# A gated feed-forward layer by seven products: gate/up parts named one product ahead, and nine block pairs instead of ten

## The chip, the cores and the metric

The kernel runs on one core of a Trainium2 chip. The metric is device time in microseconds for one execution of the whole program, a two-layer decoder trunk. Below, PE is the matrix engine, DVE the vector engine, ACT the scalar engine, POOL the general one (its queue also issues transfers), and SP the queue that issues most transfers.

## What is computed

Two layers, each a token mixer followed by a dense gated feed-forward (FFN); pre-normalisation before each, plain residual adds, one final normalisation. The prompt has 1024 tokens and there are 8 single decode tokens, so every matrix product runs over 1032 columns. All is float32. The part that the change touches, cut to what matters:

```python
D_MODEL = 1024
D_FF = -(-8 * D_MODEL // (3 * 256)) * 256          # 2816 = 22 blocks of 128

def swiglu(x, w_gate_up, w_down):
    g, u = jnp.split(x @ w_gate_up, 2, axis=-1)
    return (jax.nn.silu(g) * u) @ w_down

for layer in range(DEPTH):                         # layer 0: mLSTM mixer, layer 1: latent attention
    ...                                            # mixer, residual add
    hp = hp + swiglu(rmsnorm(hp, norm_ffn[layer]), ffn_w_gate_up[layer], ffn_w_down[layer])
    hs = hs + swiglu(rmsnorm(hs, norm_ffn[layer]), ffn_w_gate_up[layer], ffn_w_down[layer])
y_prompt = rmsnorm(hp, norm_final)
```

## The kernel before

**Precision.** A float32 operand is split into a rounded high half and the rest (`split`: ACT writes the high half, DVE subtracts for the low half), and each product is three matmuls: high x high, high x low, low x high (`mm3`, lines 134 to 136). So every weight and every activation passes through ACT and DVE before PE can use it.

**Tiling.** The 1032 columns are two parts, i = 0 with 2 x 256 columns and i = 1 with 2 x 260. The hidden dimension is 22 blocks f of 128. `gate_up(wg, f, parts)` makes one block of gated activations `u[f, i]`, as a 2 x 2 block product in seven instead of eight products (`PRODUCTS`). Per product and part it issues 4 x 3 = 12 matmuls into a bank tagged `sc`. The weights' operands of the seven products come from the generator `operands`: two loads of 512 KB (tag `wr`, two buffers, one for gate and one for up), four sums and differences on POOL (tag `S`), and seven splits (`put`). The split parts go to three slots in turn: two of tag `wh` and one of tag `w3`. They are named in the order of the products, each just before the product that uses it, but for one (`s1`) that is named a product early.

**Pairs.** `down` multiplies pairs of blocks (f0, f0 + 1) with the down weights, again by seven products. A pair is four items (two output tiles of 128 each), an item is 14 steps (7 products x 2 parts) of 3 matmuls, in banks `mm` and `ss`. Each item loads its weights (`dr`, 256 KB, on SP), makes sums and differences on DVE (`dS`), splits them (tags `dA` to `dD`), evicts its products into a staging tile, and ends with two accumulating stores into the residual `x_d`, issued by POOL: from the tile `st` (part 1) and from `st0` (part 0), which lies in the two `wl` buffers of the weights' pool. The activations of a pair are combined and split into fourteen tiles `b` by `spread`, at steps listed in `SPREAD`.

**Order.** `ffn` first makes blocks 2, 0 and 1 (0 and 1 for part 0 were made before), then starts the generator `down` and gives it to `gate_up` for blocks 3 to 21: after every second k of a product one step of `down` follows, 28 steps for a block. So from block 3 on, PE alternates six matmuls of gate/up with three of a pair. Ten pairs are done so; the last two blocks, 20 and 21, are kept as split activations `act` and multiplied plainly, with 3 matmuls per block, output tile and column piece, in the tail: `last_products`, called by `to_mla` in layer 0 (three pieces of 344 columns) and by `finish` in layer 1 (384, 384 and 264). The tail loads the down weights of the kept blocks for each of the 8 output tiles (`wr`, 128 KB), splits them, reads the residual back from `x_d`, adds, and goes on to the next layer's operands and squares or to the final normalisation and the output. In layer 1 block 21 is made in two passes, part 0 and part 1, each with its own loads.

The program is traced in this order and placed on the engines' queues by the framework when it is built; each queue then runs in order, with semaphores between engines. A tile's slot in a pool must be read out before its next owner may be written.

**Memory.** Pools are stacks on the left and the right of the on-chip memory. `fp` (left) holds what the pairs need: the `b` tiles, `dr`, `dS`, `dA` to `dD`, `st`, and `w3`. `gu` (right) holds `u`, `gt` and `S`; `fc` (right) the normalised inputs of part 1; `fz` (left) those of part 0.

Of the kernel before, what the change touches and what calls it, by code (L numbers as in the profile page):

```python
# [91 lines left out]
class Kern:  # L92
# [896 lines left out]
    def operands(self, wg, f):  # L989
        nc = self.nc  # L990
        A = []
        for c0 in (f * P, DFF + f * P):
            raw = self.t(self.wp, [P, KT * P], "wr")
            nc.sync.dma_start(raw.rearrange("p (k m) -> p k m", m=P), self.wsrc(wg, 0, KT, c0, P))
            A.append(raw.rearrange("p (k r m) -> p r k m", r=2, m=P))
        (a11, a12), (a21, a22) = ((x[:, 0], x[:, 1]) for x in A)

        def put(x):
            self.no += 1
            pool, tag = (self.wp, "wh") if self.no % 3 else (self.fp, "w3")  # L1000
            w = self.t(pool, [P, KT * P], tag, F32R).rearrange("p (i k m) -> p i k m", i=2, m=P)
            self.split(w[:, 0], w[:, 1], x)
            return w

        G = nc.gpsimd.tensor_tensor
        s, s3 = (self.t(self.gu, [P, 4, P], "S", bufs=2) for i in range(2))
        G(s, a21, a22, op=ALU.add)  # L1007
        G(s3, a11, a21, op=ALU.subtract)
        yield put(a11)
        yield put(a12)  # L1010
        s1 = put(s)
        G(s, s, a11, op=ALU.subtract)  # L1012
        yield put(s)
        yield s1
        G(s, a12, s, op=ALU.subtract)  # L1015
        yield put(s3)
        yield put(a22)
        yield put(s)


    def gate_up(self, wg, f, parts, down=iter(()), skip=0, steps=1):
        nc = self.nc
        V = nc.vector
        gu = self.gu
        banks = {}
        U, X = {}, {}
        for (s, bank, first), w in zip(PRODUCTS, self.operands(wg, f)):
            for i in parts:
                pw = PW[i]
                if (i, bank) not in banks:  # L1030
                    banks[i, bank] = self.mmt("sc")[:, :pw]
                ps = banks[i, bank]
                xh, xl = self.F[i][s]
                for k in range(4):
                    self.mm3(ps, w[:, 0, k], w[:, 1, k], xh[:, k], xl[:, k], bool(first) and k == 0, k == 3, skip_group_check=True)
                    if k % 2:
                        if skip:
                            skip -= 1
                        else:
                            for _ in range(steps):  # L1040
                                next(down, None)
                if s == 0:
                    U[i] = self.rows(f, i)
                    X[i] = self.t(gu, [P, PW[1]], "gt", bufs=2)[:, :pw]
                u, x = U[i], X[i]
                if s == 0:
                    nc.scalar.copy(u[:, 0], ps)
                elif s == 4:
                    V.tensor_tensor(u[:, 0], u[:, 0], ps, op=ALU.add)
                    nc.scalar.activation(u[:, 0], u[:, 0], AF.Silu)  # L1050
                elif s == 3:
                    nc.scalar.copy(x, ps)
                elif s == 2:
                    nc.scalar.copy(u[:, 1], ps)
                    V.tensor_tensor(u[:, 1], u[:, 1], banks[i, 1], op=ALU.add)
                elif s == 5:
                    V.tensor_tensor(u[:, 0], u[:, 0], ps, op=ALU.mult)  # L1057
                elif s == 6:
                    V.tensor_tensor(x, x, ps, op=ALU.add)
                    nc.scalar.activation(x, x, AF.Silu)  # L1060
                    V.tensor_tensor(u[:, 1], u[:, 1], x, op=ALU.mult)
# [42 lines left out]
    def down(self, wd):  # L1104
        nc = self.nc
        V = nc.vector
        todo = [(f0, dp) for f0 in range(0, NF - 2, 2) for dp in range(KT // 2)]
        src = self.down_raw(wd, *todo[0])
        W = {n: self.down_put(src, n) for n in "ABCD"}
        st0 = [self.t(self.wp, [P, KT * P], "wl", F32R).bitcast(F32) for _ in range(2)]  # L1110
        yield
        for n, (f0, dp) in enumerate(todo):
            more = n + 1 < len(todo)
            st, o, banks = [], [], []
            for i in range(2):
                x = st0[dp % 2].rearrange("p (r t) -> p r t", r=2) if i == 0 else self.t(self.fp, [P, 2, 2 * PW[1]], "st", bufs=2)
                st.append(x)
                o.append(x.rearrange("p r (c t) -> p r c t", c=2))
                banks.append([self.mmt(t)[:, :PW[i]] for t in ("mm", "ss")])
            for e in range(14):  # L1120
                s, k, first = PRODUCTS[e // 2]
                i = e % 2
                ps = banks[i][k]
                w, j = PARTS[s]
                w, b = W[w][:, :, j], self.B[s, i]
                self.mm3(ps, w[:, 0], w[:, 1], b[:, 0], b[:, 1], bool(first), True, skip_group_check=True)
                c = o[i]
                if s == 0:
                    nc.scalar.copy(c[:, 0, 0], ps)
                elif s == 4:  # L1130
                    V.tensor_tensor(c[:, 0, 0], c[:, 0, 0], ps, op=ALU.add)
                elif s == 3:
                    nc.scalar.copy(c[:, 0, 1], ps)
                elif s == 2:
                    nc.scalar.copy(c[:, 1, 1], ps)
                    V.tensor_tensor(c[:, 1, 1], c[:, 1, 1], banks[i][1], op=ALU.add)
                elif s == 5:
                    nc.scalar.copy(c[:, 1, 0], ps)
                elif s == 6:
                    V.tensor_tensor(c[:, 0, 1], c[:, 0, 1], ps, op=ALU.add)  # L1140
                    nc.gpsimd.dma_start(self.x_d[:, 2 * dp:2 * dp + 2, 512 * i:512 * i + 2 * PW[i]], st[i], accum_op=ALU.add)  # L1141
                if more and e == 0:
                    src = self.down_raw(wd, *todo[n + 1])
                if more and e in (6, 9, 12, 13):
                    x = {6: "A", 9: "B", 12: "D", 13: "C"}[e]
                    W[x] = self.down_put(src, x)
                for f, z in ((f0, dp * 14 + e + 56), (f0 + 2, dp * 14 + e)):
                    if 0 < f < NF - 2:
                        for when, x, part in SPREAD:
                            if when == z:  # L1150
                                self.spread(f, x, part)
                yield

    def ffn(self, layer):
        wg, wd = self.ffn_w_gate_up[layer], self.ffn_w_down[layer]
        self.fp = self.pool("ffn")
        self.B = {}
        for _, x, i in SPREAD:
            if i == 0:
                self.spread(0, x, i)  # L1160
        self.gate_up(wg, 2, (0, 1))
        self.gate_up(wg, 0, (1,))
        self.gate_up(wg, 1, (1,))
        for _, x, i in SPREAD:
            if i == 1:
                self.spread(0, x, i)
        g = self.down(wd)
        next(g)
        self.gate_up(wg, 3, (0, 1), g, 1, 2)
        for f in range(4, NF - 1):  # L1170
            self.gate_up(wg, f, (0, 1), g)
        fs = range(NF - 2, NF)
        self.act = {}

        def last(pool, tag, i):
            for f in fs:
                if f not in self.act:
                    self.act[f] = [self.t(pool, [P, T], tag(f - NF + 2, x), F32R) for x in range(2)]
                o = lambda x: x[:, 512 * i:512 * i + 2 * PW[i]].rearrange("p (c t) -> p c t", c=2)
                self.split(o(self.act[f][0]), o(self.act[f][1]), self.u[f, i], lo_eng=self.nc.vector)  # L1180

        if layer:
            for i in range(2):
                self.gate_up(wg, NF - 1, (i,), g)
                last(self.fz, lambda j, x: f"f{2 * j + x}l", i)
            self.fc.release()
        else:
            self.gate_up(wg, NF - 1, (0, 1), g)
            self.fc.release()
            self.lt = self.pool("lt", side="right")  # L1190
            for i in range(2):
                last(self.lt, lambda j, x: f"l{j}{x}", i)
        for _ in g:
            pass
        return wd, fs


# [10 lines left out]
    def to_mla(self, wd, fs):  # L1208
# [22 lines left out]
        self.lead = self.ahead(self.load_w(self.wsrc(self.mla_w_in[0], 0, KT, QL, P), KT, P), z, KT, P)  # L1231
        y = self.rms_tok(SS, T)
        tl.release()
        self.lt.release()
        self.gu.release()
        self.fp.release()
        self.rsp = self.pool("rsz")
# [780 lines left out]
```

## Time and profile before

| | us |
|---|---|
| median of 3 runs | 2785.11 (2776.23 to 2789.87) |
| profiled execution | 2787.24 |
| its span, first to last instruction | 2785.5 |
| PE busy in the span | 2579.9 (93%) |
| DVE busy | 1925.7 (69%) |
| ACT busy | 1352.1 (49%) |
| POOL busy | 859.2 (31%) |
| mean granted clock of PE | 0.962 |

The times of the profile are from the start of the span. Layer 0's FFN with its pairs runs from about 564 to 1218 and its tail to about 1263; layer 1's from about 2060 to 2731, and its tail to the end. "Busy" is the union of an engine's instruction times; a busy PE may still run at half its clock, which the granted clock shows (1.00 is full). In a row of waits the first name is the instruction that waited and the second the one that released it; in a row of groups the last number is idle time of that engine just before the group's instructions. Line 118 is the subtraction that makes a low half, line 117 the copy that makes a high half, whoever calls them, so the tile's name tells which it is: `wh`, `w` and `wl` are weights, `b` a pair's activations.

### The profile page before, as it was taken

What the parts mean: (1) busy time and instruction counts of PE and PEld (TensorE: products, weight loads), DVE (VectorE), ACT (ScalarE), POOL (GpSimd) and SP (SyncE); (2) the same over time, 40 slices, a digit from 0 to 9 for tenths busy, and PEclk for the clock granted to TensorE, in tenths of its full rate; (3) what the DMA queues carried; (4) which work ended last, traced back from release to release, by engine and by line L of the source; (5) the groups of instructions that cost most, each with busy time, mean ns of one, the idle gap of its engine ahead of it and who ended that gap; (6) DMA issues with size and microseconds to landing.
All of it is one profiled execution on the core that took longest, in us unless ns stands there. A gap on an engine that the chain in (4) does not pass through costs nothing.

```text
span 2785.5 us, 55009 instructions
## 1 busy us (share of the span) xinstructions
PE 2579.9 (93%) x21199; PEld 2412.7 (87%) x21199; DVE 1925.7 (69%) x4469; ACT 1352.1 (49%) x3403; POOL 859.2 (31%) x778
## 2 busy tenths in 40 slices
PE   8999998889999999989889899888989999999987
PEld 8998977889999999988876767677988999999987
DVE  4345678967777777776558677685777777777776
ACT  4212334445555555553345464555446555555553
POOL 1001002233333333332336454442213333333333
PEclk9999989999999999999989999899999999999998
DMA  5133555327555566663667776555425566555665
GB/s 183 38 76 92 132 142 146 108 62 140 120 116 113 113 120 120 127 173 102 216 220 272 242 257 219 199 202 180 130 75 108 117 121 117 116 113 119 123 129 145
DMA packets 346508, 392.91 MB, mean 141 GB/s; under 512 B 23833, under 2 KB 275102, under 8 KB 337926
## 3 DMA queue, kind: packets, MB, share of 16 engines
q0 software_dynamic: 63872, 191.79, 30.0%
q1 hardware_dynamic: 257974, 181.25, 21.9%
q10 hardware_dynamic: 24400, 16.36, 2.4%
q8 instruction: 166, 2.72, 0.4%
q14 instruction: 96, 0.79, 0.1%
HBM read 255.17 MB, written 134.16 MB: 140 GB/s over the span
## 4 chain that ended last, share of the span: by engine, by line
PE 55%; DVE 24%; DMA 9%; ACT 4%; issue 4%; POOL 3%; SPq 0%; POOLq 0%; DVEq 0%; ACTq 0%
PE sc L136 10%; PE sc L134 10%; PE sc L135 10%; PE mm L134 4%; PE mm L136 4%; PE mm L135 4%; DVE b L118 3%; DVE tt L1796 2%; PE ss L1828 2%; DMA Gb<-G_d 2%; PE ss L134 1%; PE ss L136 1%; PE ss L135 1%; DVE wl L118 1%; DVE wh L118 1%
## 5 line engine op out<-in xcount | busy, mean ns | idle before, releaser
L117 ACT ACTIVATE wh<-wr 128x512 fp32r<-128x512 f32 (+3 forms) x176 | 139.1, 790 | 225.6 <-PE mm L135 130.9
L1141 POOL DMA_DIRECT2D x_d<-wl x80 | 96.4, 1205 | 317.7 <-DVE wl L1140 231.6
L1796 DVE STREAM_TRANSPOSE tt<-nat 128x1024 f32<-128x1024 f32 x128 | 153.7, 1222 | 14.6 <-DMA nat<-in_cache_latent_dram,idx 8.3
L1007 POOL TENSOR_TENSOR S<-wr 128x512 f32<-128x512 f32 x45 | 67.2, 1493 | 245.5 <-DMA wr<-in_ffn_w_gate_up_dram 229.3
L1012 POOL TENSOR_TENSOR S<-S,wr 128x512 f32<-128x512 f32 x45 | 63.1, 1402 | 246.9 <-DVE wh L118 171.5
L118 DVE TENSOR_TENSOR b<-u,b 128x256 fp32r<-128x256 f32 (+1 forms) x280 | 126.2, 456 | 18.0 <-ACT b L117 18.0
L117 ACT ACTIVATE b<-u 128x256 fp32r<-128x256 f32 (+1 forms) x280 | 109.1, 415 | 45.8 <-DVE u L1057 19.6
L118 DVE TENSOR_TENSOR wl<-wr,wh 128x1024 fp32r<-128x1024 f32 (+2 forms) x83 | 100.8, 1216 | 43.6 <-ACT wh L117 28.9
L1141 POOL DMA_DIRECT2D x_d<-st x80 | 109.1, 1363 | 11.8 <-ACT b L117 10.3
L1015 POOL TENSOR_TENSOR S<-wr,S 128x512 f32<-128x512 f32 x45 | 75.8, 1685 | 119.6 <-DVE wh L118 79.2
L134 PE MATMUL mm<-zh,wh 128*128 128x344 f32 x320 | 104.5, 326 | 5.9 <-DVE ot L462 5.9
L118 DVE TENSOR_TENSOR wh<-S,wh 128x512 fp32r<-128x512 f32 x121 | 86.4, 714 | 33.9 <-ACT wh L117 32.8
L135 PE MATMUL mm<-zl,wh 128*128 128x344 f32 x320 | 103.5, 324 | 0.0
L136 PE MATMUL mm<-zh,wl 128*128 128x344 f32 x320 | 103.3, 323 | 0.0
L1803 PE MATMUL ss<-tt,qbd 128*32 128x128 f32 x2560 | 88.7, 280 | 9.6 <-DVE tt L1796 7.9
L117 ACT ACTIVATE wh<-S 128x512 fp32r<-128x512 f32 x121 | 76.2, 630 | 39.7 <-PE sc L136 22.1
L1090 DVE TENSOR_TENSOR dS<-dr 128x128 f32<-128x128 f32 x80 | 52.1, 651 | 62.1 <-DMA dr<-in_ffn_w_down_dram 59.9
L1803 PEld LDWEIGHTS ss<-tt,qbd 128*32 128x32 f32 x2560 | 71.3, 112 | 23.1 <-DVE tt L1796 17.6
L1699 PE MATMUL mm<-wh,vt 128*128 128x256 f32 (+1 forms) x320 | 78.6, 307 | 9.9 <-ACT wh L117 5.0
L118 DVE TENSOR_TENSOR wh<-wr,wh 128x512 fp32r<-128x512 f32 x91 | 69.0, 758 | 23.4 <-ACT wh L117 22.8
L134 PE MATMUL sc<-zh,wh 128*128 128x344 f32 x256 | 84.1, 329 | 0.2 <-DVE q L432 0.2
L135 PE MATMUL sc<-zl,wh 128*128 128x344 f32 x256 | 83.1, 325 | 0.0
(1026 smaller groups left out, 11106.1 us busy)
## 6 DMA issues: line engine op xcount, KB each, us to landing
wr<-in_ffn_w_gate_up_dram SPq DMA_DIRECT2D x98, 512.0 KB
x_d<-st POOLq DMA_DIRECT2D x80, 520.0 KB, 8.4
x_d<-wl POOLq DMA_DIRECT2D x80, 512.0 KB, 6.2
dr<-in_ffn_w_down_dram SPq DMA_DIRECT2D x80, 256.0 KB
wr<-in_mlstm_w_in_dram SPq DMA_DIRECT2D x24, 512.0 KB
wr<-in_mlstm_w_out_dram SPq DMA_DIRECT2D x16, 512.0 KB
wr<-in_mla_w_o_dram SPq DMA_DIRECT2D x15, 512.0 KB
q<-qn_d SPq DMA_DIRECT2D x28, 256.0 KB
```

Source lines behind the costliest of these rows:

```text
L117: ins = nc.scalar.activation(hi, src, AF.Copy)
L118: self.low = e.tensor_tensor(lo, src, hi.bitcast(F32), op=ALU.subtract)
L134: mm(ps, wh, xh, start=start, stop=False, **kw)
L135: mm(ps, wh, xl, start=False, stop=False, **kw)
L136: self.last = mm(ps, wl, xh, start=False, stop=stop, **kw)
L1007: G(s, a21, a22, op=ALU.add)
L1012: G(s, s, a11, op=ALU.subtract)
L1015: G(s, a12, s, op=ALU.subtract)
L1141: nc.gpsimd.dma_start(self.x_d[:, 2 * dp:2 * dp + 2, 512 * i:512 * i + 2 * PW[i]], st[i], accum_op=ALU.add)
L1699: nc.tensor.matmul(o, x, y, start=i == 0, stop=i == len(ops) - 1)
L1796: V.transpose(out=tt, in_=src.rearrange("p s (c i) -> p c s i", i=32))
L1803: nc.tensor.matmul(psS[32 * j:32 * j + 32, u * P:u * P + P], self.qbd[:, b, cb], tt[:, c, 4 * j:4 * j + 4].rearrange("p s k -> p (s k)"), ...
```

## The change

Four edits, all in the FFN.

1. In `gate_up`, the generator `operands` is asked for one part more before the first product, and then for the next part before each product: every split is named one product earlier. The order of the seven products, their matmuls and the slots stay.
2. `w3`, the third slot of the parts, moves from `fp` to `gu`, since `fp` now ends before the last two blocks.
3. `down` runs over nine pairs (blocks 0 to 17) instead of ten. With 504 steps for 502 places, its last two steps follow block 19.
4. Blocks 18 to 21 are kept for the tail. After the last pair, `fp` is released and a new pool in its place holds the eight tiles of kept halves, 4 blocks x high and low. Blocks 18 and 19 are split first, then blocks 20 and 21 are made with no steps of `down` between their products, and each is split when it is made. The kept halves lay before in `fz` (layer 1) or in a pool `lt` on the right (layer 0), which is gone. The tail's code is the same; with four blocks it loads 256 KB of weights per output tile and issues 12 matmuls where it issued 6.

```diff
@@ operands
-            pool, tag = (self.wp, "wh") if self.no % 3 else (self.fp, "w3")
+            pool, tag = (self.wp, "wh") if self.no % 3 else (self.gu, "w3")
@@ gate_up
-        for (s, bank, first), w in zip(PRODUCTS, self.operands(wg, f)):
+        ops = self.operands(wg, f)
+        ahead = next(ops)
+        for s, bank, first in PRODUCTS:
+            w, ahead = ahead, next(ops, None)
             for i in parts:
@@ down
-        todo = [(f0, dp) for f0 in range(0, NF - 2, 2) for dp in range(KT // 2)]
+        todo = [(f0, dp) for f0 in range(0, NF - 4, 2) for dp in range(KT // 2)]
...
-                    if 0 < f < NF - 2:
+                    if 0 < f < NF - 4:
@@ ffn
-        for f in range(4, NF - 1):
+        for f in range(4, NF - 2):
             self.gate_up(wg, f, (0, 1), g)
-        fs = range(NF - 2, NF)
...
         for _ in g:
             pass
+        self.fp.release()
+        self.fp = self.pool("ffn2")
+        fs = range(NF - 4, NF)
+        self.act = {f: [self.t(self.fp, [P, T], "a%d%d" % (f % 4, x), F32R) for x in range(2)] for f in fs}
+
+        def keep(f, i):
+            o = lambda x: x[:, 512 * i:512 * i + 2 * PW[i]].rearrange("p (c t) -> p c t", c=2)
+            self.split(o(self.act[f][0]), o(self.act[f][1]), self.u[f, i])
+
+        for f in fs[:2]:
+            for i in range(2):
+                keep(f, i)
+        for f in fs[2:]:
+            for parts in ((0,), (1,)) if layer and f == NF - 1 else ((0, 1),):
+                self.gate_up(wg, f, parts)
+                for i in parts:
+                    keep(f, i)
+        self.fc.release()
         return wd, fs
@@ to_mla
-        self.lt.release()
```

More of the change, by code (lines that the diff above doesn't have):

```diff
@@ L1169, in ffn @@
         self.gate_up(wg, 3, (0, 1), g, 1, 2)
-        for f in range(4, NF - 1):
+        for f in range(4, NF - 2):
             self.gate_up(wg, f, (0, 1), g)
-        fs = range(NF - 2, NF)
[L1173 to L1192, printed above, removed]
         for _ in g:
             pass
+        self.fp.release()
[14 more added lines that the diff above has]
+        self.fc.release()
         return wd, fs
```

## The prediction

> **What bounds the kernel now.** I read the head of the page first, then busy time by stretch of the two FFN stages, then the waits of each stretch, and last the instructions around the longest waits. Columns of the stretches: length, busy us (and count) of PE, PEld, DVE, ACT, POOL, granted clock, DMA share, GB/s.
>
> ```profile
> span 2785.5 us, 55009 instructions
> PE 2579.9 (93%) x21199; PEld 2412.7 (87%) x21199; DVE 1925.7 (69%) x4469; ACT 1352.1 (49%) x3403; POOL 859.2 (31%) x778
> ...
> 50.00:100.00 50.00, 50.00 (x319) 50.00 (x318) 12.50 (x21) 4.24 (x4) 0.00 (x0) 1.00 0.20 51
> ...
> 2350.00:2400.00 50.00, 50.00 (x423) 50.00 (x422) 36.29 (x83) 27.41 (x74) 15.81 (x12) 1.00 0.61 122
> ...
> 640.00:1218.00 578.00, 563.68 (x4644) 555.25 (x4644) 426.23 (x1029) 325.41 (x886) 195.61 (x146) 1.00 0.61 121
> 1218.00:1263.50 45.50, 32.58 (x155) 29.26 (x153) 37.07 (x63) 24.95 (x56) 20.22 (x20) 0.81 0.72 206
> ...
> 2120.00:2692.00 572.00, 555.15 (x4535) 545.95 (x4534) 422.78 (x1018) 318.96 (x871) 195.02 (x145) 0.99 0.61 118
> 2692.00:2731.00 39.00, 33.06 (x229) 31.71 (x229) 22.44 (x44) 16.71 (x44) 10.78 (x10) 0.87 0.78 187
> 2731.00:2746.50 15.50, 10.77 (x38) 8.80 (x37) 7.92 (x14) 4.96 (x13) 5.49 (x5) 0.67 0.82 187
> 2746.50:2776.00 29.50, 27.58 (x194) 25.21 (x192) 22.44 (x48) 10.96 (x24) 13.61 (x15) 1.00 0.29 108
> ```
>
> The long interleaved stretches (640 to 1218 in the first layer, 2120 to 2692 in the second) are TensorE's: it is busy 97% of them. The tails are not: 1218 to 1263.5 is the first layer's, with PE busy 32.6 of 45.5 us at a granted clock of 0.81; from 2731 on is the second's, with a bad first third and then 27.6 of 29.5 us busy.
>
> Two paces come from rows in which PE never rests. 50 us / 423 = 0.118 us for a matmul of 256 or 260 columns (the second FFN), and 50 us / 319 = 0.157 us for one of 344 columns (the first projection). Durations of single matmuls overlap and are not used.
>
> Which waits stand in those stretches (us in all, times, longest), first 640 to 1200, then 2120 to 2690, the first tail, and 2692 to 2731:
>
> ```profile
> PE sc L136 <- DVE wh L118: 6.0, 5, 1.2
> PE sc L136 <- DVE w L118: 3.6, 3, 1.2
> PE ss L134 <- DVE st L1140: 1.8, 8, 0.2
> ...
> PE sc L136 <- DVE wh L118: 6.0, 5, 1.2
> PE sc L136 <- DVE w L118: 3.6, 3, 1.2
> ...
> PE sc L136 <- DVE wl L118: 8.8, 4, 3.7
> PE sc L134 <- ACT wh L117: 3.4, 3, 1.7
> ...
> PE mm L134 <- ACT wl L1135: 2.6, 1, 2.6
> PE sc L134 <- ACT wh L117: 2.4, 1, 2.4
> PE mm L134 <- ACT st L1138: 0.7, 1, 0.7
> PE sc L136 <- DVE wh L118: 0.2, 1, 0.2
> ```
>
> In each interleaved stretch eight waits of 1.2 us are for the low half of a gate/up part, one per pair of feed-forward blocks. Their place:
>
> ```profile
> 784.09 0.63 ACT L117 ACTIVATE w<-S 128x512 fp32r<-128x512 f32 x1
> ...
> 783.49 0.41 DVE L1140 TENSOR_TENSOR st<-st,ss 128x260 f32<-128x260 f32 x1
> ...
> 788.73 0.68 DVE L118 TENSOR_TENSOR w<-S,w 128x512 fp32r<-128x512 f32 x1
> ...
> 2728.11 0.42 ACT L117 ACTIVATE wh<-wr 128x256 fp32r<-128x256 f32 x1 [0.35 <-PE sc L136]
> ...
> 2730.90 0.43 ACT L1060 ACTIVATE gt<-gt 128x260 f32<-128x260 f32 x1
> ```
>
> The high half was ready at 784.7, and the low half came 4 us later, from a DVE that had not paused. The last two rows show that the queues do not follow the order of naming strictly: a tail weight's split stands ahead of the Silu of the last block, which was named before it. So naming a part earlier raises its precedence; it does not by itself move it.
>
> **The change, part by part.** First the stores of the pairs, from the page's list of DMA issues:
>
> ```profile
> x_d<-wl POOLq DMA_DIRECT2D x80, 512.0 KB, 6.2
> ```
>
> *A pair less.* The row counts 40 items of a pair and two output tiles per layer; 36 stay. 4 items x 14 steps x 3 matmuls = 168 per layer, 168 x 0.118 = 19.9 us off TensorE, which bounds that stage: -19.9 per layer, -39.8. With them go 4 item loads on SP, 8 accumulating stores on POOL, and on DVE and ACT the evictions, the item's splits and the spreading of that pair; all lay beside PE. The small waits of that pair (the L1140 row and its like, some 0.5 us a pair) give -1 in both layers together.
>
> *Two blocks more in the tail.* 8 output tiles x 3 pieces x 2 more factors x 3 = 144 matmuls per layer. At 0.157 us (the second layer's pieces are 384, 384 and 264 wide, the same 1032 columns) that is 22.6 us of work, so on PE alone a layer loses 22.6 - 19.9 = 2.7 us. What counts is how much of it falls into time that is idle now.
>
> First layer's tail: 45.5 us for 144 x 0.157 = 22.6 us of products and little more; the rest is the two waits above, 12.2 us, and the lowered clock. What DVE does there:
>
> ```profile
> L118 DVE TENSOR_TENSOR wl<-wr,wh 128x256 fp32r<-128x256 f32 x7 | 5.8, 839 | 1.1 <-DMA x_d<-wl 1.1
> ...
> L121 DVE SCALAR_TENSOR_TENSOR f3l<-x,g,f3h 128x344 fp32r<-128x344 f32 x3 | 3.4, 1137 | 0.0
> ```
>
> Residual adds and low halves keep DVE busy 37.1 us and stay as they are; only the weight's low half doubles (128x512), by at most 8 x 0.84 = 6.7 us, to 43.8. PE will have 288 x 0.157 = 45.2 us. So PE becomes the longest, just ahead of DVE; with some waits left I take 51 us: +5.5. Ends: +0 (45.5) and +22.6 (nothing fills).
>
> Second layer's tail: from 2746.5 it is PE's already, so work there comes on top. The first 15.5 us hold a wait and a low clock:
>
> ```profile
> PE sc L136 <- DVE wl L118: 3.8, 1, 3.8
> ...
> 2731.93 5.88 DMA x_d<-wl
> ```
>
> The second weight's low half lies in a buffer from which the last accumulating store reads until it lands. After the change those stores land two blocks earlier (2 x 168 x 0.118 = 40 us), so the wait has no cause: 3.8 us, and 15.5 x (1 - 0.67) = 5.1 us of clock, go. Late next is the weights' load, now 256 KB for each output tile through the two raw buffers; its cover is 12 x 0.157 x 384/344 = 2.1 us of products per tile. I take 22.6 - 8.9 = +13.7; ends +8 (more idle filled) and +22.6.
>
> *Last blocks without cover.* Blocks 20 and 21 now run with no pair step between their products. In both layers 24 matmuls (2.8 us) per part hide the splits, about 0.63 on ACT and 0.68 on DVE. The second layer runs block 21 in two passes, with 12 matmuls (1.4 us) per part; its like is the passes for blocks 0 and 1 before the first pair:
>
> ```profile
> PE sc L134 <- ACT w L117: 3.3, 1, 3.3
> ...
> 589.17 0.70 DVE wh L118
> 589.89 5.46 DMA wr<-in_ffn_w_gate_up_dram
> 595.50 1.31 POOL S L1007
> ...
> 598.68 1.40 POOL S L1012
> 600.10 0.64 ACT w L117
> 600.78 0.58 PE sc L134
> ...
> 601.00:606.50 5.50, 5.50 (x27) 5.50 (x28) 3.40 (x5) 1.89 (x5) 1.29 (x1) 0.51 0.32 95
> ```
>
> There the second raw load starts when its buffer's last split is done, and load, sum, split, difference and split take 10.9 us in a chain (589.89 to 600.78). The wait was 3.3 us, and 5.5 us at clock 0.51 lost another 2.7: 6.0. I charge that once (between the two passes), and 1 us at the entry to the first. Now the same passes lose 2.6 + 2.4 + 0.9 = 5.9 us of waits in 2692 to 2731 and 39 x 0.13 = 5.1 us of clock, 11.0, because the loads queue on SP behind reads of the accumulated residual. So 7.0 - 11.0 = -4. Ends -11 and +4.
>
> [...]
>
> *Naming one ahead.* It adds no instruction. In the interleaved stretch the late low half gains the precedence of a whole product (some 4 us, 36 x 0.118), against the 1.2 us that it is late: 9.6 us per layer to gain. Behind it on DVE stand the evictions of the down banks, 0.42 us each, and PE waits for those already (the L1140 row). I let them take 2.6 back: -7 per layer, -14. Ends: -19.2, and +11 if each of 16 such places costs one low half, 0.69. In the start passes I count nothing: the chain above begins with a buffer coming free, which no naming changes.
>
> *Keeping the four activations.* Eight splits in place of the spreading of a pair and of four splits; they need the last pair's factors to be read out, since they lie in that memory, and block 20 cannot write its first result before block 18 is kept. Two products (5.7 us) pass before PE needs that, so I cost it at nothing; without that cover it is one split, 1.3 us per layer. The third weight slot's new place costs nothing.
>
> **Sum** against the profiled execution, 2787.2 us (2785.5 of span and 1.7 around it): -39.8 - 1 + 5.5 + 13.7 - 4 - 14 = -39.6, so 2747.6. The median of the runs lies 2.1 us lower: **2745 us**, 1.4% below.
>
> **The rivals.**
>
> *The naming changes nothing*, because the planner had hoisted what it could: and most parts start on ACT when a slot falls free, as this one does, 1.26 us idle and then released by PE:
>
> ```profile
> 763.51 0.63 ACT L117 ACTIVATE wh<-S 128x512 fp32r<-128x512 f32 x1 [1.26 <-PE sc L136]
> ```
>
> Then the 14 is missing: 2760. Against it: the late low half waits for DVE, not for a slot.
>
> *The tails take all of the new work*, since DVE is nearly as long as PE in the first and the weights' loads pace the second: + 17.1 + 8.9, giving 2771. For it: the 43.8 against 45.2.
>
> *Slower: early parts hold up evictions.* Blocks 3 to 19 have 119 parts per layer, 238 in all. If an early split delays a down bank by d each time and PE feels it, the time moves by 238 x d while the 14 is lost: -25.6 + 238 d. From d = 0.11 the gain is gone; at 0.2 us it is 2807. Against it: the L1140 waits are 0.2 us and eight in a stage, and DVE rests between them; for it: DVE at 74% in that stage, in strict order.
>
> *Better*: the first tail at its 46 us, and the second filling more: 2730.
>
> **How the numbers follow.** Forecast 0.45 (own range 2735 to 2758), better 0.07, naming void 0.17, tails in full 0.19, slower 0.12. About 0.5%, 14 us, is what a measurement of this kernel can tell from no change (its three runs spread over that). Below 2771: 0.45 + 0.07 + 0.17 + a quarter of the tails case = 0.74; within 0.14; slower 0.12. The range leaves out the slower case and the lowest few: 2722 to 2782.
>
> **What would show it.** The pair: 72 accumulating stores of each kind for 80. The naming: the two L136 rows gone from the interleaved stretch, and the L1140 row not above 4 us. First tail: PE busy above 85% of about 51 us, clock near 1. Second: no wait for `wl` at its start, about 68 us from the last block to the end. Block 21's second pass: one wait of 3 us on ACT. The forecast is wrong if new waits on `st`, `ss` or `mm` appear through the stage, or if the tails wait on weights.

## The result and the profile after

The changed kernel takes 2736.82 us (median of four runs, 2733.56 to 2737.95) against 2780.67 us for the kernel before on the same chip: ratio 0.984, interval 0.9804 to 0.9876. The forecast was 2745 (2722 to 2782). Two runs of later kernels, 10255 us and 3471 us at clocks of 0.22 and 0.65, are left out of their ratios. Below, TensorE, VectorE, ScalarE and GpSimd are the engines that the profile calls PE, DVE, ACT and POOL. First the head of the page, and its row for the stores of the pairs:

```profile
span 2735.1 us, 54524 instructions
...
PE 2553.6 (93%) x21151; PEld 2398.4 (88%) x21151; DVE 1884.8 (69%) x4321; ACT 1320.8 (48%) x3287; POOL 824.9 (30%) x762
...
x_d<-wl POOLq DMA_DIRECT2D x72, 512.0 KB, 6.2
```

72 stores for 80: the ninth pair is the last. 48 matmuls fewer (336 less 288), as counted. PE's share of the span stayed at 93%: work and idle time fell together.

Busy time by stretch (columns as before: length, PE, PEld, DVE, ACT, POOL, clock, DMA share, GB/s). The rows are, in the first layer, most of the interleaved stretch, then blocks 20 and 21, then the tail; in the second, blocks 20 and 21, and the start and rest of the tail:

```profile
640.00:1149.00 509.00, 500.20 (x4136) 493.77 (x4136) 388.99 (x915) 287.89 (x786) 170.86 (x132) 1.00 0.62 121
1149.00:1194.00 45.00, 41.88 (x339) 41.67 (x338) 21.18 (x40) 17.61 (x39) 10.88 (x8) 0.96 0.32 72
1194.00:1240.00 46.00, 46.00 (x294) 46.00 (x294) 33.15 (x60) 27.84 (x56) 17.36 (x18) 1.00 0.70 224
...
2615.70:2669.80 54.10, 43.60 (x340) 42.16 (x339) 29.25 (x48) 22.47 (x47) 15.92 (x13) 0.97 0.51 139
...
2669.80:2685.30 15.50, 14.65 (x80) 13.30 (x79) 9.31 (x16) 7.11 (x14) 4.47 (x4) 1.00 0.54 166
2685.30:2735.10 49.80, 42.54 (x302) 41.17 (x300) 25.26 (x56) 12.57 (x26) 15.15 (x16) 0.94 0.23 86
```

The first tail, 45.5 us with PE busy 32.6, has become 46 us in which PE never rests, with twice the products. The start of the second tail went from 10.8 of 15.5 us busy at clock 0.67 to 14.7 of 15.5 at 1.00. Blocks 20 and 21 are what now has holes: 3.1 us and 10.5 us.

The waits: the first layer's interleaved stretch, then blocks 20 and 21 of the first and of the second layer:

```profile
PE ss L134 <- DVE wl L1143: 1.7, 3, 0.8
PE ss L134 <- DVE st L1143: 1.6, 7, 0.2
PE ss L134 <- DVE st L1134: 1.5, 7, 0.2
PE sc L136 <- DVE wh L118: 1.3, 5, 0.5
...
PE mm L134 <- ACT wl L1138: 1.1, 2, 0.5
PE sc L136 <- DVE w L118: 0.5, 2, 0.3
...
PE sc L134 <- ACT u L1050: 3.1, 1, 3.1
...
PE sc L134 <- ACT wh L117: 6.0, 2, 4.3
PE sc L134 <- ACT u L1050: 3.1, 1, 3.1
```

The two L136 rows, 9.6 us before (8.4 of them up to 1149), are 1.8; the waits for the down banks (`ss` and `mm`), 5.9 us here and 4.7 in the second layer, are the larger part now. One of their rows is new: `st` at L1134, 1.5 us in each layer. The 3.1 us on `u`, once in each layer, is new.

To see where the time went, each profiled execution is cut at landmarks on TensorE. "Pairs" is from the first product of the first gate/up part to the last pair step, "alone" is blocks 20 and 21 without a pair (before they ran among pair steps), "tail" is from there to the next stage, or to the end. In us:

| kernel | pairs 1 | alone 1 | tail 1 | pairs 2 | alone 2 | tail 2 | both FFN |
|---|---|---|---|---|---|---|---|
| before | 742.9 | – | 73.6 | 752.7 | – | 54.5 | 1623.7 |
| after | 675.0 | 44.9 | 73.0 | 669.1 | 53.9 | 65.5 | 1581.4 |
| after, again | 674.7 | 45.0 | 72.9 | 668.7 | 56.4 | 66.0 | 1583.7 |
| after, third chip | 673.5 | 45.0 | 72.9 | 667.1 | 54.1 | 64.8 | 1577.5 |
| naming alone | 736.2 | – | 70.9 | 742.5 | – | 55.9 | 1605.6 |
| all but naming | 681.8 | 43.4 | 73.0 | 675.8 | 58.4 | 65.4 | 1597.7 |
| own `u` tiles | 674.2 | 45.0 | 72.9 | 668.2 | 54.0 | 65.6 | 1579.9 |
| keeping later | 672.5 | 41.3 | 73.0 | 668.0 | 51.3 | 65.7 | 1571.8 |
| one pass | 677.3 | 46.1 | 72.9 | 668.2 | 43.4 | 66.6 | 1574.5 |
| both of these | 673.4 | 41.4 | 72.9 | 667.1 | 41.3 | 66.0 | 1562.2 |

The FFN stages account for 42.3 us of the 50.4 by which the profiled span fell. Another 7.1 lie in the stage between the two FFNs, which the diff does not touch: it took 686.8 us in the profile before, 679.7 in that after, and 696 to 709 in the executions of the later kernels that are timed here. It drifts with no change of its code, so times of different chips are not compared, and the table is read by its FFN columns.

### The profile page after: what moved, and what is told of

Read it like the earlier page. It is cut to its first block, busy times and chain, and to the rows that moved or that the text cites. A ratio compares the mean times of both kernels' runs of the same rounds, so it can differ in the third digit from the quotient of the medians.

```text
span 2735.1 us, 54524 instructions
## 1 busy us (share of the span) xinstructions
PE 2553.6 (93%) x21151; PEld 2398.4 (88%) x21151; DVE 1884.8 (69%) x4321; ACT 1320.8 (48%) x3287; POOL 824.9 (30%) x762
## 5 line engine op out<-in xcount | busy, mean ns | idle before, releaser
L117 ACT ACTIVATE wh<-wr 128x512 fp32r<-128x512 f32 (+2 forms) x176 | 141.4, 804 | 224.4 <-PE mm L135 129.5
L1144 POOL DMA_DIRECT2D x_d<-wl x72 | 86.7, 1204 | 315.3 <-DVE wl L1143 250.0
L118 DVE TENSOR_TENSOR b<-u,b 128x256 fp32r<-128x256 f32 (+1 forms) x252 | 135.5, 542 | 16.7 <-ACT b L117 16.7
L117 ACT ACTIVATE b<-u 128x256 fp32r<-128x256 f32 (+1 forms) x252 | 98.4, 415 | 43.0 <-DVE u L1060 15.4
L136 PE MATMUL mm<-zh,wl 128*128 128x344 f32 x320 | 103.3, 323 | 0.0
L1144 POOL DMA_DIRECT2D x_d<-st x72 | 99.9, 1388 | 7.0 <-ACT b L117 6.1
L1802 PEld LDWEIGHTS ss<-tt,qbd 128*32 128x32 f32 x2560 | 70.9, 111 | 21.5 <-DVE tt L1795 15.9
L1698 PE MATMUL mm<-wh,vt 128*128 128x256 f32 (+1 forms) x320 | 76.9, 302 | 10.7 <-ACT wh L117 6.0
L850 POOL TENSOR_TENSOR ss<-ss,sq 128x512 f32<-128x512 f32 (+2 forms) x36 | 49.5, 1374 | 113.4 <-ACT sq L849 113.1
L136 PE MATMUL sc<-zh,wl 128*128 128x344 f32 x256 | 82.9, 324 | 0.0
```

What stands on the lines that cost most here:

```text
L117: ins = nc.scalar.activation(hi, src, AF.Copy)
L118: self.low = e.tensor_tensor(lo, src, hi.bitcast(F32), op=ALU.subtract)
L136: self.last = mm(ps, wl, xh, start=False, stop=stop, **kw)
L850: (V if d == KT - 1 else nc.gpsimd).tensor_tensor(SS[:, cs], SS[:, cs], sq, op=ALU.add)
L1698: nc.tensor.matmul(o, x, y, start=i == 0, stop=i == len(ops) - 1)
L1802: nc.tensor.matmul(psS[32 * j:32 * j + 32, u * P:u * P + P], self.qbd[:, b, cb], tt[:, c, 4 * j:4 * j + 4].rearrange("p s k -> p (s k)"), ...
```

## The experiments

Kernels of one group share a chip. Ratios are to the kernel before, run beside them.

**The change again, its naming alone, and all of it but the naming.** Unchanged kernel:

> The changed kernel again, beside the parts of the change on one chip. From its first runs: ratio to the kernel before 0.984, that is 42 to 45 us less. In the two profiles the first layer's FFN with its tail took 24.6 us less and the second's 18.7 us less, 43.3 us together; the rest of the profile's difference lay outside the FFN and should not come back.

Measured: 2762.13 against 2794.85 us, ratio 0.988 (0.986 to 0.99): 32.7 us, less than the 42 to 45 expected, while the FFN columns (1583.7) come back within 2.3 us. With a third chip, below, the change is worth 43.9, 32.7 and 42.8 us. Then the kernel before with the naming only:

```diff
-        for (s, bank, first), w in zip(PRODUCTS, self.operands(wg, f)):
+        ops = self.operands(wg, f)
+        ahead = next(ops)
+        for s, bank, first in PRODUCTS:
+            w, ahead = ahead, next(ops, None)
```

> Naming one ahead alone, with ten pairs and two kept blocks. Theory (the part waits shrink and the down banks' waits grow): PE's gaps over 0.3 us in the pairs' stage were 18.4 us before 1149 and 13.6 after the whole change in the first layer, so naming alone gives 4 to 5 us per layer, 8 to 10 in all, ratio 0.9965; in the stage the late low halves wait 3 to 4 us in all for 9.6, and the waits on st and wl rise from 3 to 6 us. First rival, the naming is void because the planner had hoisted all it could: ratio 1.000 and the 1.2 us waits stay. Second rival, the prediction's own figure: 14 us, ratio 0.995.

And the changed kernel with these lines turned back:

> Nine pairs and four kept blocks without naming ahead. Theory: the pairs give what the whole change gives less the naming, 33 to 36 us, ratio 0.9877, with eight waits of 1.2 us on late low halves still in each layer's stage, and tails like those of the changed kernel (the first without waits at a full clock, the second 65 us). Rival, the parts need each other (blocks 20 and 21 have no pair steps between their products, so without naming ahead each product there waits for its split): waits on wh and w of 1 us per product in blocks 20 and 21, some 15 to 25 us over both layers, ratio 0.995.

Measured: the naming alone 2781.49 us, 0.9954 (0.9937 to 0.9972); all but the naming 2776.82 us, 0.9928 (0.991 to 0.9946). The two gains, 0.46% and 0.72%, add up to the 1.2% of the whole. The theory of 8 to 10 us for the naming was too low, the prediction's 14 us, named there as a rival, was right; nine pairs without the naming gave 18.0 us where 33 to 36 were expected. In the FFN columns the naming is worth 18.1 us on the kernel before, and 14.0 when added to the rest (1597.7 to 1583.7); 7.1 us lie in the pairs of each layer. Against the row of before, which is from another chip, the columns show 5 to 8 us more than the times do (18.1 for 13.4, 26.0 for 18.0, 40.0 for 32.7); within this chip the two agree (14.0 and 14.7). Waits of the first interleaved stretch, with the naming alone, and then with all but the naming:

```profile
PE ss L134 <- DVE st L1143: 1.7, 8, 0.2
PE ss L134 <- DVE st L1134: 1.7, 8, 0.2
...
PE sc L136 <- DVE wh L118: 1.3, 5, 0.6
...
PE sc L136 <- DVE w L118: 0.5, 3, 0.2
```

```profile
PE sc L136 <- DVE wh L118: 6.0, 5, 1.2
PE sc L136 <- DVE w L118: 2.4, 2, 1.2
PE ss L134 <- DVE st L1140: 1.5, 7, 0.2
PE mm L134 <- ACT wl L1135: 1.1, 2, 0.5
PE ss L134 <- DVE wl L1140: 1.1, 2, 0.8
```

The late low halves go with the naming and stay without it, and the bank waits grow from 3.7 us to 5.9 in the changed kernel.

**The 3.1 us wait at block 20.** ScalarE in the changed kernel, around that wait (start, length, idle before and its releaser in brackets):

```profile
1152.24 0.63 ACT L117 ACTIVATE w<-S 128x512 fp32r<-128x512 f32 x1 [2.71 <-PE sc L136]
1155.09 0.63 ACT L117 ACTIVATE wh<-S 128x512 fp32r<-128x512 f32 x1 [2.22 <-PE sc L136]
1155.63 2.19 ACT L117 ACTIVATE a<-u 128x512 fp32r<-128x512 f32 x4
1157.72 0.63 ACT L1050 COPY u<-sc 128x256 f32<-128x256 f32 x2
```

The eviction of block 20's first bank (L1050), for which the third product waits, comes behind the four splits that keep blocks 18 and 19 (`a<-u`). Either it must, since it writes the `u` that they read, or it only stands behind them in ScalarE's order. First, tiles of their own for blocks 20 and 21:

```diff
-        x = self.t(self.gu, [P, 2, PW[1]], "u%d%d" % ((1, 0) if (f, i) == (0, 1) else (f % 2, i)))[:, :, :PW[i]]
+        own = f >= NF - 2
+        k = (f % 2, i) if own else (1, 0) if (f, i) == (0, 1) else (f % 2, i)
+        x = self.t(self.fp if own else self.gu, [P, 2, PW[1]], "u%d%d" % k)[:, :, :PW[i]]
```

> The changed kernel with result tiles of their own for blocks 20 and 21, in the pool of the kept halves. In the changed kernel PE waits 3.1 us in each layer, at the third product of block 20, for the copy of its first product, and the clock halves after it. Theory (that copy stands behind the keeping of block 18, whose result tile it overwrites): the wait goes in both layers, 6 to 9 us less than the changed kernel with the clock. Rival (the memory of the kept halves comes free late, after the pairs' last stores, and the new tiles lie in the same memory): the wait stays, no difference.

Measured: 2758.04 us, 0.9872 (0.9849 to 0.9895), as the changed kernel beside it (0.988). The wait is still there:

```profile
PE sc L134 <- ACT u L1052: 3.1, 1, 3.1
```

So the `u` that the copies read was not the cause; the new tiles lie in the memory that the pairs gave up, which could still come free late. Next, with the same tiles, the four keeping splits are named behind block 20:

```diff
-        for f in fs[:2]:
-            for i in range(2):
-                keep(f, i)
         for f in fs[2:]:
             for parts in ((0,), (1,)) if layer and f == NF - 1 else ((0, 1),):
                 self.gate_up(wg, f, parts)
+                for j in fs[:2] if f == NF - 2 else ():
+                    for i in range(2):
+                        keep(j, i)
```

> The changed kernel, with own result tiles for blocks 20 and 21 and blocks 18 and 19 kept only after block 20 is named. Own tiles alone left the 3.1 us wait where it was, so its cause is not the overwritten tile. Theory: in ACT's strict order the four keeping copies (2.2 us in one run) stand between a split of block 20 that waits for its slot and the copy of block 20's first product. With the keeping named later the wait falls from 3.1 to about 1.0 us (a split of 0.63 and a copy of 0.35), and the half clock behind it goes: 2 to 4 us less per layer than the changed kernel, best seen in the stretch from the last pair step to the tail (45.0 us in the first layer). Rival (the pool's memory comes free late on the chip itself): the wait stays above 2.5 us, since the new tiles lie in that memory too.

Measured: 2759.29 us beside 2799.43, 0.9853 (0.9816 to 0.989); the interval takes in the changed kernel, so this effect is read from the profile. Blocks 20 and 21 of the first layer, and the wait that is left there:

```profile
1146.10:1187.40 41.30, 40.26 (x338) 40.05 (x337) 21.11 (x40) 17.40 (x39) 10.85 (x8) 1.00 0.35 77
```

```profile
PE sc L134 <- ACT u L1052: 1.0, 1, 1.0
```

The wait falls from 3.1 to 1.0 us, and the stretch of the first layer from 45.0 to 41.3: 2.1 of wait and 1.7 of half clock. The tiles lie in the same memory as in the run above, so neither it nor `u` was what the eviction waited for: the cost was its place behind the four splits in ScalarE's order.

**Block 21 of the second layer in one pass.** The changed kernel with one line:

```diff
-            for parts in ((0,), (1,)) if layer and f == NF - 1 else ((0, 1),):
+            for parts in ((0, 1),):
```

> The changed kernel with block 21 made in one pass in the second layer too. Theory (with 12 matmuls per part the chain load, sum, split, difference, split is not covered, 4.1 to 4.3 us at the second pass and 1.6 us at the first, plus half clock): the stretch from the last pair step to the tail goes from 54 to 56 us to 46 to 48, and the tail stays at 65 to 66 us: 7 us less. Rival (the two passes were hiding the tail's loads, which need the inputs of part 0 read out): the tail grows by 4 us or more and the sum stays within 3 us.

Measured: 2750.51 us, 0.982 (0.9791 to 0.9849). Its blocks 20 and 21 of the second layer, and their waits:

```profile
2642.00:2685.40 43.40, 40.27 (x339) 40.07 (x338) 21.87 (x43) 19.13 (x43) 11.00 (x9) 1.00 0.49 119
```

```profile
PE sc L134 <- ACT u L1050: 3.1, 1, 3.1
```

The 6.0 us of waits on `wh` are gone, and the stretch is 10.5 to 13 us shorter than in the three executions of the changed kernel, where 7 were expected. The tail behind it is 66.6 us against 64.8 to 66.0: little of it is given back.

**Both together** (later keeping, one pass):

> The changed kernel with blocks 20 and 21 in activation tiles of their own, the keeping copies of blocks 18 and 19 named after block 20, and block 21 of the second layer in one pass. Theory (the two waits are separate and each costs its wait and the low clock behind it): the gains of the two edits alone add, -3.5 us in each layer at block 20 and -11 us at block 21, so the two FFN stages together come to 1563 to 1570 us, and the time is 14 to 19 us below the changed kernel's, ratio to the kernel before 0.978 to 0.982. Rival (the start of the tail is limited by the weight loads, so what is won at block 21 is lost there again): the FFN stages stay at 1572 to 1576 us, and the second tail grows from 66 to over 72 us.

Measured, with the changed kernel on the same chip: 2741.92 us against 2757.83, and 2800.64 before; ratios 0.9799 (0.9781 to 0.9817) and 0.9862 (0.9842 to 0.9881). The two stretches:

```profile
1145.50:1186.80 41.30, 40.26 (x338) 40.05 (x337) 21.00 (x41) 17.15 (x39) 10.87 (x8) 1.00 0.36 81
2631.30:2672.50 41.20, 40.16 (x337) 39.95 (x336) 20.90 (x39) 16.55 (x37) 10.99 (x9) 1.00 0.58 149
```

Both are now 41.2 us, with 1.0 us of them idle. The FFN stages come to 1562.2 us, 15.3 below the changed kernel's on that chip, and the time is 15.9 below: the theory's sum. By its ratio this is the fastest version of the study. The changed kernel on that chip was run under this expectation:

> The changed kernel once more, on the chip of the next two. Both theories: ratio to the kernel before 0.984 to 0.988, the two FFN stages together 1581 to 1584 us.

**What the tails' new products cost.** The changed kernel without the products of blocks 18 and 19 in both tails, timed once:

```diff
-        for js in (range(len(fs) - 1), (len(fs) - 1,)):
+        for js in (range(2, len(fs) - 1), (len(fs) - 1,)):
...
-                    self.mm3(ps, w[0][:, j], w[1][:, j], ah[:, cs], al[:, cs], j == 0, j == len(fs) - 1)
+                    self.mm3(ps, w[0][:, j], w[1][:, j], ah[:, cs], al[:, cs], j == 2, j == len(fs) - 1)
```

> The changed kernel with the products of blocks 18 and 19 left out of the tail, 144 matmuls (22.6 us) per layer; their weights are loaded and split all the same, and the output lacks their part. Theory (the first tail is paced by DVE and transfers when PE has only two blocks, so two more fill idle time; the second is PE's own but for its first third): the first tail with what follows it, 73 us, falls by 3 to 8 us only, the second, 65.5 us, by 12 to 16. Rival (the new tail is free of waits because the pairs' stores have landed long before, and the products are paid in full): both fall by 20 us or more.

Measured: 2735.04 us; first tail 68.7 us in place of 72.9, second 52.1 in place of 65.5. The products' part of the first tail:

```profile
1188.30:1234.20 45.90, 34.97 (x179) 32.77 (x177) 40.52 (x66) 29.24 (x60) 19.55 (x18) 0.85 0.72 239
```

The same 22.6 us of products cost 4.2 to 4.3 us in the first tail, where without them PE idles 10.9 of 45.9 us at clock 0.85, and 13.4 in the second. The 13.4 is the less certain: blocks 20 and 21 just before that tail took some 57.5 us in this run, 53.9 to 56.4 in the changed kernel.

**The wait at the start of the old second tail.** The prediction gave it to the last accumulating store, which still reads the weight's buffer. The kernel before, with all weights of the last output tiles in `fw`:

```diff
-            if d < 2:
-                W.append(self.load_w(src, len(fs), P))
-                continue
```

> The kernel before, with all weights of the last output tiles in the two tiles that the third one used already, instead of the first two in the slots of the block weights, one of which the last accumulating store still reads. Theory (the 3.8 us wait at the start of the second tail, and the low clock behind it, come of that store alone): the wl wait goes, the second tail falls from 54.5 us by 6 to 9 us, the two FFN stages together from 1624 to 1615 to 1618 us, ratio to the kernel before 0.996 to 0.998. Rival (the weight's load and its place in the queues set it): a wait of 3 us or more stays there under another name (fw), and the second tail falls by less than 3 us, ratio 0.999 to 1.001. With only two tiles for three early weights, a wait of up to 2 us on fw could also come later in the tail.

Measured: 2795.98 us, 0.9979 (0.9965 to 0.9993). The second tail takes 54.4 us, as with 54.5 before, and waits twice for weights:

```profile
PE mm L134 <- ACT fw L117: 3.1, 1, 3.1
...
PE sc L134 <- ACT fw L117: 2.8, 1, 2.8
```

with ScalarE idle ahead of each of these splits, for the weight's own load:

```profile
2751.33 0.42 ACT L117 ACTIVATE fw<-wr 128x256 fp32r<-128x256 f32 x1 [2.21 <-DMA wr<-in_ffn_w_down_dram]
...
2756.01 0.42 ACT L117 ACTIVATE fw<-wr 128x256 fp32r<-128x256 f32 x1 [3.85 <-DMA wr<-in_ffn_w_down_dram]
```

So the store was not alone: the buffer freed, the load of the next weights takes the wait over, in a stretch where the DMA engines are 79% busy (82% before). The kernel before shows it too: there the third weight's split starts at 2738.20, after 3.65 us of waiting for its load, 0.4 us behind the low half that waited for the store. The expectation's remark on two tiles is a mistake: the code gives each output tile a tile `fw{d}` of its own, so none of these waits is for one of them to come free. The small gain of the run lies elsewhere: the first tail is 71.5 us for 73.6, and the rest is not explained.

**Less work for VectorE in the interleaved stretch.** Its bank waits grew; do they fall if GpSimd takes three of the four subtractions that spread a pair?

```diff
-        V = G = self.nc.vector
+        V, G = self.nc.vector, self.nc.gpsimd
```

> The changed kernel with three of the four differences of a pair's spreading (t1, t3, t4: six instructions per pair of 0.42 us on DVE) on POOL. Theory (what is left of PE's waits in the pairs' stage, some 13 us of gaps per layer, comes from DVE's backlog while a pair is spread): 2.5 us less DVE work in each backlog, the waits on st and wl shrink by a third or more, 3 to 6 us less over both layers. Rival (POOL takes about 0.75 us for such an instruction, slows DVE's own beside it, and the differences are a chain): no gain, or 5 to 15 us more with longer DVE instructions.

Measured: 2821.36 us, 1.0063 (1.0034 to 1.0093): slower. From the first gate/up product to the last pair step, the first layer takes 702.7 us, where the changed kernel, run again, took 674.7. VectorE runs 53 instructions fewer there (1087 for 1140) and is busy no less (515.8 us for 513.1). In the interleaved part, GpSimd's longest subtraction, and VectorE's low halves, here and in the changed kernel:

```profile
L1078 POOL TENSOR_TENSOR u<-u,u 128x256 f32<-128x256 f32 (+1 forms) x16 | 17.0, 1065 | 0.9 <-DVE u L1074 0.9
```

```profile
L118 DVE TENSOR_TENSOR wh<-S,wh 128x512 fp32r<-128x512 f32 x43 | 35.4, 823 | 6.9 <-ACT wh L117 6.7
```

```profile
L118 DVE TENSOR_TENSOR wh<-S,wh 128x512 fp32r<-128x512 f32 x44 | 30.2, 687 | 5.2 <-ACT wh L117 4.5
```

GpSimd takes 1065 ns for a subtraction that takes VectorE some 420 ns, and VectorE's low halves take 823 ns for 687. The waits of that same span, from its first product on:

```profile
PE sc L134 <- ACT wh L117: 19.3, 9, 3.9
PE sc L136 <- DVE wh L118: 10.7, 7, 3.2
```

The `ss` rows have gone, as wanted, but the parts' high and low halves are late by 30.0 us in place of 10.8 (6.6 and 4.2 in the changed kernel). In all, PE is idle 19.5 us longer, and busy 8.4 us longer with the same matmuls, at a granted clock of 0.97 for 0.98. So 4.7 to 5.9 us of bank waits a layer were bought too dear. Whether the parts are late because GpSimd also makes their raw sums, or because VectorE's operations grow, was not separated.

## Why the prediction was right

The total was right to 8 us, and the sum by its own profiled execution to 3 (-39.6 for -42.3 in the FFN stages). Three chips give 43.9, 32.7 and 42.8 us, 39.8 on average. The naming and the removed pair came as counted. Two other steps were wrong by 9 us each, in opposite directions, so that the sum came out this near is in part luck.

*A pair less, blocks 20 and 21 alone, keeping.* Predicted -39.8 - 1 - 4 = -44.8. All but the naming against before: 742.9 to 681.8 + 43.4, and 752.7 to 675.8 + 58.4: -17.7 and -18.5, so -36.2. The pair itself went as counted: the first layer's column of pairs fell by 61.1 us, for 504 matmuls fewer in it (the pair's 168 and the 336 of blocks 20 and 21), which at 0.118 us are 59.5. So the 8.6 us are missing in blocks 20 and 21 and the keeping, where the 336 matmuls are 39.6 us of work and took 43.4 and 58.4. The second layer's stretch, without the naming (a row as in the table by stretch):

```profile
2657.60:2716.00 58.40, 46.88 (x338) 45.86 (x337) 26.87 (x48) 22.25 (x47) 16.91 (x13) 0.85 0.47 128
```

Two terms failed. Keeping was costed at nothing because two products (5.7 us) would cover it: it cost 3.1 us of waiting in each layer, and in the profile after 1.7 more of half clock in the first. The step asked when the data were due, and not what stands ahead of the eviction in ScalarE's queue: part splits that wait for a slot (2.71 and 2.22 us idle in the rows above) and then 2.2 us of keeping. The other term is block 21 in two passes. Its passes were charged 7.0 us, one stall of 3 us among them; the second stretch lost 18.8 us, 15.7 without the wait on `u`, of which 6.6 are the same matmuls at a lower clock (PE busy 46.9 us for 40.3). In the profile after, with the naming, there are still two waits of 6.0 us, the longest 4.3, and 11.2 us lost. For the old passes 11.0 were credited, and the second layer's column of pairs fell by 76.9 us, 17.4 more than its 504 matmuls. So of the gain of 4 some 1.7 are left, and the one-pass run shows that the two passes cost 10.5 us or more. Both sides of this term were too small, and that they nearly cancel is luck.

*Tails.* Predicted +5.5 and +13.7; measured -0.6 and +10.9 without the naming (-0.6 and +11.0 with it). The first tail's step held VectorE to 43.8 us and PE just above it. It was busy 33.2 us. Its rows there:

```profile
L118 DVE TENSOR_TENSOR wl<-wr,wh 128x512 fp32r<-128x512 f32 (+1 forms) x8 | 6.2, 777 | 0.5 <-ACT wh L117 0.4
...
L121 DVE SCALAR_TENSOR_TENSOR f3l<-x,g,f3h 128x344 fp32r<-128x344 f32 x3 | 1.7, 577 | 1.3 <-ACT f3h L120 1.3
```

The doubled low half takes no longer than the single one (777 ns for 839), and `f3l` takes 577 ns for 1137, now waiting for ScalarE each time. (777 mixes in one of 128x1024; the seven of 128x512 average 712.) The durations of before were not costs of the operation: in the tail without the new products they come back at the same shapes (the row mixes in two of 128x1024; the seven of 128x512 average 888 ns), and never waiting:

```profile
L118 DVE TENSOR_TENSOR wl<-wr,wh 128x512 fp32r<-128x512 f32 (+1 forms) x9 | 8.7, 962 | 0.0
...
L121 DVE SCALAR_TENSOR_TENSOR f3l<-x,g,f3h 128x344 fp32r<-128x344 f32 x3 | 3.3, 1110 | 0.0
```

So the step that failed took a duration from a crowded stretch for a constant; what ran beside the long ones is taken up in the last section. PE at 100% of 46 us at clock 1.00 is the rival "better" in this one stage. Nor is filled idle time all of it: without the new products the first tail is 4.9 us shorter than before (68.7 for 73.6; its waits for `wl` are 4.6 us for 8.8), and they cost 4.3. What shortened it was not tested.

The second tail: +13.7 was put together from 22.6 less 8.9. Without the new products it is 2.4 us shorter than before, and they cost 13.4 of their 22.6. So the +11.0 is near the +13.7 for reasons only partly those given: its start gained what was said (10.77 to 14.65 us busy, clock to 1.00), and more idle time was filled elsewhere, but the store was not the only thing that the weights waited for.

*Naming.* Predicted -14, with nothing in the start passes: -14.0 on top of the rest, and -18.1 alone, where the tails change by -2.7 and +1.4 as well. From the first gate/up product to the first pair step it is 87.5 us with the naming and 87.7 without. The 2.6 us that evictions were to take back are 2.2 in the first layer's rows of waits (3.7 to 5.9). The rival that it does nothing and the slower one are both out: with 7 waits each of 0.2 us on `st`, d is nowhere near 0.11.

*By its signs.* The stores, the L136 rows (1.8 us, not quite gone), the L1140 row (L1143 now: 1.6) and the first tail came as said; the second stretch from the last block to the end is 65.5 us for 68. The sign for block 21 did not hold, and the wait on `u` was on no list. One sign of being wrong did appear: the `st` row at L1134 is a new wait through the stage, but it is 1.5 us a layer, too small to turn the sum.

## What to carry to other kernels

Ask of each moved step not only when its data are due, but what it stands behind in its engine's order: four splits of low urgency named ahead of an eviction cost 3.1 us of waiting in each layer, and naming them later left 1.0. Durations read in a crowded stretch are not constants (`f3l` took 1137 ns before and 577 after); for a stage that changes its bound, take them from a quiet stretch too. Work that moves into a tail costs little where the tail idles (4.3 of 22.6 us in the first), and more where it idles less (13.4 in the second).

## What the runs showed of the hardware

The half clock came in steps of 3.413 us. In the profiles before and after, all 63 of its spells begin at whole multiples of 3.413 us from one another, to within 10 ns, and each lasts one to six such steps, but for the last of each profile, which runs past its end. In the profile after, TensorE around the 3.1 us wait of the first layer (two rows) and around the same wait in the second (three rows), cut at these steps:

```profile
1155.28:1158.70 3.42, 0.58 (x4) 0.58 (x5) 2.94 (x5) 3.07 (x7) 0.00 (x0) 1.00 1.11 190
1158.70:1162.11 3.41, 3.41 (x18) 3.41 (x17) 0.83 (x3) 1.13 (x3) 0.00 (x0) 0.50 0.64 175
2619.62:2623.03 3.41, 2.09 (x18) 1.88 (x16) 1.24 (x2) 1.23 (x3) 1.95 (x2) 1.00 1.08 157
2623.03:2626.45 3.42, 1.62 (x13) 1.62 (x14) 3.22 (x7) 2.53 (x7) 0.00 (x0) 1.00 1.09 208
2626.45:2629.86 3.41, 3.41 (x31) 3.41 (x30) 0.69 (x1) 1.42 (x4) 0.00 (x0) 1.00 0.33 99
```

In the first layer the wait fell into one step, PE was busy 0.58 of 3.42 us there, and the next step ran at 0.50. In the second it straddled two, PE busy 2.09 and 1.62 us in them, and the clock stayed at 1.00. Over the two profiles, a step at full clock in which PE was less than 40% busy was followed by one at half clock in 33 of 35 cases (the other two lie in the first 3 us of a program), one 45 to 55% busy in 3 of 19, and one 80% busy or more in 8 of 1339. The same wait of 3.1 us thus cost 1.7 us more in the first layer and nothing in the second; in the kernel without the naming the first layer's stretch is 43.4 us for 45.0 (PE busy 40.3 us for 41.9), which is that difference.

VectorE's low halves took longer beside GpSimd's additions and subtractions. With GpSimd's subtractions added, those of 128x512 rose from 687 to 823 ns (above), while the bank evictions kept 418 ns in the same run:

```profile
L1143 DVE TENSOR_TENSOR st<-st,ss 128x260 f32<-128x260 f32 x33 | 13.8, 418 | 10.5 <-PE ss L136 10.5
```

One by one, in the first interleaved stretch of the kernel before, the changed one and the one with GpSimd's subtractions: the parts' low halves of 128x512 take 674 to 694 ns wherever none of GpSimd's additions or subtractions runs beside them (307 of them), and 1080, 1161 and 1578 ns on average where one covers half of their time or more (19, 10 and 19; single ones 679 to 1797 in the kernel before). The evictions into `st` take 408 to 427 ns either way. In the first tail GpSimd makes 18 additions in each kernel, so it is their place that changed: before, 12 of the 23 low halves of 128x344 had one beside them for half their time and took 801 to 1318 ns, the others 565 to 577; after, only one of 22 did (1253 ns), most met one for their last 150 ns or so, and those 21 took 565 to 579. The weights' low halves of 128x256 that had read 839 ns took 411 alone and up to 1148 beside an addition.

No run here takes GpSimd's work away, so these rows show what ran side by side and not the cause.
